# Projections over four PSUM banks, zeroing tied to the last norm, and an earlier retention in a two-layer hybrid transformer

## The chip, the cores and the metric

The kernel runs on one core of one Trainium2 chip. The metric is the device time of one execution in microseconds; the median of three runs is given. The engines are TensorE (PE, with its weight loads PEld), VectorE (DVE), ScalarE (ACT), GpSimd (POOL) and SyncE (SP, which here only issues loads and stores). Each engine runs its own instructions in the order in which they were laid down when the program was built; semaphores hold an instruction back until its inputs are there, and what stands behind it on that engine waits too.

## The reference

Two layers on 512 tokens of width 1024. Each layer mixes three kinds of attention and then runs a feed-forward part. Cut to its core:

```python
def hybrid_layer(x, attn_norm_w, w_in, ret_norm_w, kv_norm_w, w_uk, w_uv, w_out, mlp_norm_w, w_up, w_down, pos):
    h = rms_norm(x, attn_norm_w)
    proj = h @ w_in
    ret_cols, dsa_cols, dil_cols = jnp.split(proj, _offsets((RET_COLS, DSA_COLS, DIL_COLS)), axis=-1)
    mixed = jnp.concatenate([retention_mixer(ret_cols, ret_norm_w, pos),       # 4 heads, chunks of 128
                             dsa_mixer(dsa_cols, kv_norm_w, w_uk, w_uv),       # 4 heads, top-128 keys by an indexer
                             dilated_mixer(dil_cols)], axis=-1)                # 8 heads, three dilation patterns
    x = x + mixed @ w_out
    h = rms_norm(x, mlp_norm_w)
    return x + jnp.square(jax.nn.relu(h @ w_up)) @ w_down

def reference(x, ...):
    for layer in range(DEPTH):      # DEPTH = 2
        x = hybrid_layer(x, ...)
    return rms_norm(x, final_norm_w)
```

## The kernel before

**Arithmetic.** Every fp32 matrix is split into a high part (fp32r) and a low part (what the cast left over); a product is three fp32r matmuls: high by high, high by low, low by high. Weights are loaded in chunks of up to 512 KB (`dma`, line 248), cast on ScalarE (line 278) and their low part is taken on VectorE or GpSimd (line 286); there are three raw buffers and five finished ones. The feed-forward product with `w_down` is done with seven products in place of eight (`mlp`, line 949).

**Tokens.** The 512 tokens are four tiles of 128 (t = 0 to 3). `norm` (line 376) scales one tile: ScalarE squares it with a running sum (line 361), VectorE adds the two half sums (line 364), GpSimd raises the sum to the power -1/2 (line 368; the result is `r`), VectorE or GpSimd multiply (lines 383, 387, 389), TensorE transposes (line 352), and ScalarE and VectorE write high and low part of the activation (lines 399, 400). At the very start `start` (line 1060) loads the first norm's weight row and x tile 2, then the first constants, and then, in turn, weight chunks and the other x tiles, all on SyncE's queue. It runs the norms in the order 2, 3, 0, 1.

**PSUM.** There are eight banks: two called `mm` for projections and output parts, four called `at` for scores, transposes and attention values, two called `rt` for the retention and the feed-forward. A projection (`proj`, line 791) makes 24 matmuls into one `mm` bank, and VectorE and ScalarE copy the bank out (`evac_q`, `evac_k`: lines 423, 424, 436, 438; the high half of K also crosses partitions by a DMA that ScalarE issues, line 437). `dil_v` (line 537) makes the V of four dilated heads for the four token tiles: two tiles into `mm`, two into `rt`.

**The attention stage** (`attention`, line 830). First the projections that need tokens in rows and the latent (`token_parts`), then `zeros` (line 814), five GpSimd instructions that fill the retention's state and half of each of two K tiles with zeros, then the indexer, the first of 16 rounds of top-k on VectorE (lines 602, 603), and the first V. After that a loop over h = 0 to 12 issues the scores and softmax of head h (0 to 7 dilated, 8 to 11 sparse), one group of `FILL` (projections as filler: q and k of a pair, s for a sparse q, g for the retention's gates, d for the second V, r for the retention's q and k, v and w for the latent's k and v), from h = 9 on up to three output parts (`out_part`, line 892: 12 matmuls each with half of the rows of `w_out`), the values of head h - 1, a number of retention steps, and top-k rounds. `RET` (line 54) says how many of the retention's twelve steps follow each head: three steps for each token tile, the first with its scores (lines 659 to 679), the second with its products, state and norm (lines 681 to 733), the third with its gate (lines 735 to 742). `HOLD` (line 58) says from which of the eight output parts on they are kept for behind the loop. There the kept parts come, then the eight parts with the other half of `w_out`, and the next norm.

**What sets the order.** The program is handed to a scheduler that models each engine's time and takes, among the instructions that are ready, the one that comes first in program order, with the offsets of `PR` (line 72; a positive number means later). So filler moves into the holes that the scheduler sees, and each engine's order is fixed from then on.

**The end.** `final` (line 1047) norms one token tile of the last layer: one half on GpSimd (line 1052) and ScalarE (line 1054), the other on VectorE (line 1057); both halves are stored by SyncE (lines 1055, 1058). The tiles come in the order 2, 3, 0, 1.

Of the kernel before, what the change touches and what calls it, by code (L numbers as in the profile page):

```python
# [25 lines left out]
P = 128  # L26
# [26 lines left out]
    'FILL': 'q1,q2 k1 k2,g0,d g1,k3,q3 r,v s0,w,s1,',  # L53
    'RET': (0, 0, 0, 0, 0, 4, 0, 3, 0, 1, 3, 1, 0),
    'TOPK': (1, 1, 0, 4, 0, 10, 0),
    'POOL_LO': ('dv', 'o', 'sq', 'rg', 'rqk', 'dq', 'dk', 'ukv'),
    'LSPLIT': 2,
    'HOLD': 6,
    'KS': ((4, 6), (0, 2)),
# [64 lines left out]
class Kern:  # L124
# [251 lines left out]
    def norm(self, t, wb, act, room, first=False, h0=0):  # L376
# [4 lines left out]
        if not first:  # L381
            c0, c1 = halves[0]
            nc.gpsimd.tensor_tensor(hn[:, h0], self.x[t][:, c0:c1], wb[:, c0:c1], op=ALU.mult)
        r = self.norm_stats(t, None, halves)
        for h in (h0, 1 - h0):
            if h == h0 and not first:
                nc.vector.tensor_scalar(hn[:, h], hn[:, h], r[:, 0:1], None, op0=ALU.mult)
            else:
                nc.vector.scalar_tensor_tensor(hn[:, h], self.x[t][:, h * 512:(h + 1) * 512], r[:, 0:1],
                                               wb[h] if first else wb[:, h * 512:(h + 1) * 512], op0=ALU.mult,  # L390
                                               op1=ALU.mult)
            ps = self.at()
            for k in range(4):
                self.tr(ps[:, k * P:(k + 1) * P], hn[:, h, k * P:(k + 1) * P])
            psv = ps.rearrange("p (k c) -> p k c", k=4)
            for g in range(2):
                dst = act[h * 2 + g]
                hi = dst[:, 0, :, t * P:(t + 1) * P]
                nc.scalar.copy(hi, psv[:, 2 * g:2 * g + 2])
                nc.vector.tensor_tensor(dst[:, 1, :, t * P:(t + 1) * P], psv[:, 2 * g:2 * g + 2], hi.bitcast(F32),  # L400
                                        op=ALU.subtract)
# [135 lines left out]
    def dil_v(self, L, act, g):  # L537
        us = [(self.unit((L, "dv", g, k)), (k, k + 1, k + 2, k + 3)) for k in (0, 4)]
        for t in range(NT):
            ps = self.mm() if t < 2 else self.rt_bank()  # L540
            self.tform(us, act, t, ps, 256)
# [240 lines left out]
    def latent_k(self, L, pr):  # L782
# [6 lines left out]
        return self.evac_k(ps)  # L789

    def proj(self, key, act, cols=P):
        ps = self.mm()
        self.wform(self.unit(key), act, cols, ps, cols)
# [20 lines left out]
    def zeros(self):  # L814

        z = lambda o, a: self.nc.gpsimd.tensor_scalar(o, a, 0.0, 0.0, op0=ALU.mult, op1=ALU.add)
        z(self.sv.rearrange("p a c -> p (a c)"), bc(self.ident, [[0, 4], [1, P]]))
        for i in range(4):
            o = slice(64, 128) if i % 2 == 0 else slice(0, 64)
            z(self.kl[i // 2][o, i % 2, :], bc(self.ident[o], [[0, 4], [1, P]]))  # L820

# [8 lines left out]
    def attention(self, L, act):  # L830
        nc = self.nc
        A = self.A
        sc = None
        self.rt = [self.t(self.pmix, [P, 2, 1024], F32, "mix") for _ in range(2)]
        self.vd, self.sg, self.ct, self.vs, self.rqk_done = {}, None, None, None, False
        self.masks = self.t(self.psc, [P, N_CST - N_C1], F32, "masks")
# [63 lines left out]
        for h in range(12 + C["SK"]):  # L900
# [20 lines left out]
            if h >= C["SK"]:  # L921
                with self.prio("hv", h):
                    self.head_v(heads[(h - C["SK"]) // 2], (h - C["SK"]) % 2)
            for _ in range(C["RET"][h] if h < 13 else 0):
                with self.prio("ret", h):
# [121 lines left out]
    def final(self, t, wb, pool, junk):  # L1047
# [6 lines left out]
        nc.scalar.activation(xs, xs, AF.Copy, scale=r[:, 0:1])  # L1054
        nc.sync.dma_start(self.out[t * P:(t + 1) * P, c0:c1], xs)
        o = self.x[t][:, d0:d1]
# [3 lines left out]
    def start(self):  # L1060
        nc = self.nc

        row = self.t(self.pt, [P, 2 * S], F32, "PT")
        nc.sync.dma_start(row[0:1, :], self.A["attn_norm_w"][0].rearrange("(o c) -> o c", o=1))
        self.x[2] = self.t(self.pv, [P, D], F32, "xv")
# [64 lines left out]
```

## Time and profile before

| | |
|---|---|
| median of 3 runs | 1236.36 us (1236.02 to 1240.37) |
| the profiled execution: device time | 1236.08 us |
| its span, first to last instruction | 1234.1 us |
| busy: TensorE, VectorE, ScalarE, GpSimd | 98%, 75%, 55%, 38% of the span |
| mean granted TensorE clock | 0.997 |

Layer 0's attention stage runs from the start to about 291 us, its feed-forward to 618; layer 1's end at about 898 and 1226. Times are microseconds from the span's start. In a timeline row the first number is the start, the second the time from the first start to the last end of the merged instructions, and the bracket at the end is the idle time before them and what ended it. A matmul counts as busy from its start to its modelled end, so that neighbours overlap.

### The profile page before, as it was taken

The page shows a single profiled execution, that of the slowest core. Times are in us where ns is not written, and L with a number is a line of the kernel's source. Part 1 is how long each engine was busy: PE and PEld are TensorE (multiplying, and loading weights), DVE is VectorE, ACT ScalarE, POOL GpSimd, SP SyncE. Part 2 cuts the span into 40 slices and gives each one's busy share as a digit, 9 for nine tenths or more (in the row PEclk, how much of TensorE's full clock was granted, in tenths as well). Part 3 has the DMA queues.
Part 4 walks back from the last instruction along what each step waited for, and adds up shares of the span by engine and source line. Part 5 has one row for each costly group of instructions (what it writes and reads, how often), then busy time and mean ns, then how long its engine had stood idle before and what let it go on. Part 6 is the DMA issues. An engine that isn't in the chain of part 4 may idle for free.

```text
span 1234.1 us, 16904 instructions
## 1 busy us (share of the span) xinstructions
PE 1207.2 (98%) x6116; PEld 1027.6 (83%) x6116; DVE 921.4 (75%) x1582; ACT 679.2 (55%) x1241; POOL 472.4 (38%) x461
## 2 busy tenths in 40 slices
PE   7999999999999999999999999999999999999997
PEld 5988888889888888888889888888898888888886
DVE  5599957776875966858866997687769668587596
ACT  6645758745644535535566456686465354354454
POOL 3453748553412304214224546664534032140232
PEclk9999999999999999999999999999999999999999
DMA  7432324215244061260153323231180622514201
GB/s 217 120 83 72 95 69 121 86 53 188 85 137 137 1 215 58 69 184 16 35 166 102 95 71 96 91 120 53 52 256 1 205 68 69 176 30 140 82 1 69
DMA packets 142180, 122.73 MB, mean 99 GB/s; under 512 B 6801, under 2 KB 114065, under 8 KB 142098
## 3 DMA queue, kind: packets, MB, share of 16 engines
q1 hardware_dynamic: 140178, 118.52, 31.9%
q10 hardware_dynamic: 1920, 3.15, 1.0%
q8 instruction: 48, 0.79, 0.3%
q14 instruction: 34, 0.28, 0.1%
HBM read 114.31 MB, written 4.19 MB: 96 GB/s over the span
## 4 chain that ended last, share of the span: by engine, by line
PE 85%; DVE 12%; ACT 1%; issue 1%; DMA 1%; SPq 0%; POOL 0%; POOLq 0%; DVEq 0%; ACTq 0%
PE mm L336 35%; PE mm L348 15%; PE rt L1036 14%; PE at L1036 7%; PE mm L1036 3%; DVE sc L603 3%; DVE top L602 3%; PE at L352 2%; PE at L491 2%; PE at L444 1%; PE at L443 1%; DVE ph L462 1%; PE at L336 1%; DVE Q L424 1%; DMA raw<-in_w_in_dram 1%
## 5 line engine op out<-in xcount | busy, mean ns | idle before, releaser
L336 PE MATMUL mm<-act,w 128*128 128x512 f32 (+2 forms) x2352 | 516.1, 377 | 3.1 <-DVE Q L424 3.1
L336 PEld LDWEIGHTS mm<-act,w 128*128 128x128 f32 x2352 | 424.4, 188 | 79.8 <-issue 3.9
L286 POOL TENSOR_TENSOR w<-raw,w 128x512 fp32r<-128x512 f32 (+1 forms) x124 | 160.0, 1313 | 99.2 <-ACT w L278 74.0
L278 ACT CAST w<-raw 128x1024 fp32r<-128x1024 f32 (+1 forms) x138 | 142.9, 1037 | 79.2 <-PE rt L1036 27.6
L1036 PE MATMUL rt<-w,U 128*128 128x512 f32 x768 | 183.2, 389 | 0.0
L286 DVE TENSOR_TENSOR w<-rd,w 128x1024 fp32r<-128x1024 f32 x112 | 144.7, 1304 | 50.0 <-ACT w L278 50.0
L286 DVE TENSOR_TENSOR w<-raw,w 128x1024 fp32r<-128x1024 f32 (+1 forms) x76 | 94.0, 1238 | 107.5 <-ACT w L278 107.2
L1036 PEld LDWEIGHTS rt<-w,U 128*128 128x128 f32 x768 | 144.1, 188 | 29.9
L993 POOL TENSOR_TENSOR st<-s 128x256 f32<-128x256 f32 x32 | 39.1, 1223 | 330.1 <-ACT s L982 325.3
L278 ACT CAST w<-rd 128x1024 fp32r<-128x1024 f32 x112 | 117.6, 1050 | 83.4 <-PE rt L1036 41.7
L348 PE MATMUL mm<-w,act 128*128 128x456 f32 (+2 forms) x576 | 118.4, 351 | 3.0 <-DVE act L400 1.8
L348 PEld LDWEIGHTS mm<-w,act 128*128 128x128 f32 x576 | 96.4, 189 | 15.2 <-DVE act L400 2.8
L348 PE MATMUL mm<-w,mix 128*128 128x512 f32 x384 | 97.3, 401 | 0.6 <-DVE Q L424 0.5
L1036 PE MATMUL at<-w,U 128*128 128x512 f32 (+1 forms) x396 | 97.7, 386 | 0.0
L304 DVE TENSOR_TENSOR rd<-rd,rd 128x1024 f32<-128x1024 f32 x64 | 94.3, 1473 | 0.5
L1036 PEld LDWEIGHTS at<-w,U 128*128 128x128 f32 x396 | 73.6, 188 | 15.0
L980 ACT ACTIVATE s<-mm 128x512 f32<-128x512 f32 x62 | 36.9, 595 | 84.2 <-PE mm L336 74.5
L348 PEld LDWEIGHTS mm<-w,mix 128*128 128x128 f32 x384 | 70.5, 190 | 15.2 <-DVE Q L424 0.9
L997 ACT CAST U<-st 128x1024 fp32r<-128x1024 f32 x32 | 33.7, 1054 | 80.9 <-POOL st L994 80.9
L991 POOL TENSOR_TENSOR st<-s,s 128x256 f32<-128x256 f32 x32 | 36.7, 1146 | 92.0 <-ACT s L982 92.0
L463 ACT ACTIVATE ph<-ph,sm 128x128 f32<-128x128 f32 (+1 forms) x96 | 53.9, 562 | 24.5 <-DVE sm L462 23.8
L998 DVE TENSOR_TENSOR U<-s,U 128x256 fp32r<-128x256 f32 x64 | 63.9, 998 | 0.0
(169 smaller groups left out, 1766.4 us busy)
## 6 DMA issues: line engine op xcount, KB each, us to landing
raw<-in_w_up_dram SPq DMA_DIRECT2D x64, 512.0 KB, 4.2
rd<-in_w_down_dram SPq DMA_DIRECT2D x32, 1024.0 KB, 5.1
raw<-in_w_in_dram SPq DMA_DIRECT2D x48, 512.0 KB, 3.9
raw<-in_w_out_dram SPq DMA_DIRECT2D x16, 512.0 KB, 3.9
xv<-in_x_dram SPq DMA_DIRECT2D x7, 512.0 KB, 4.8
KH<-KH ACTq DMA_DIRECT2D x24, 128.0 KB, 2.3
raw<-in_w_in_dram SPq DMA_DIRECT2D x8, 256.0 KB, 2.9
xd<-xv SPq DMA_DIRECT2D x4, 512.0 KB, 3.9
```

The lines of the kernel that those rows point to most:

```text
L278: self.nc.scalar.copy(hi, src)
L286: eng.tensor_tensor(lo[:, i:i + step], src[:, i:i + step], hi[:, i:i + step].bitcast(F32), op=ALU.subtract)
L304: sub = lambda o, a, b: self.nc.vector.tensor_tensor(o, a, b, op=ALU.subtract)
L336: self.nc.tensor.matmul(ps[:cols, toks[0]:toks[1]], a, b, start=(k == 0 and j == 0), stop=(k == KB - 1 and j == 2))
L348: self.nc.tensor.matmul(ps[:, :w], a, b, start=(n == 0), stop=(n == tot - 1))
L463: nc.scalar.activation(p, p, AF.Exp, bias=a, scale=-1.0, accum_out=b)
L602: nc.vector.max(m, sc[b])
L603: nc.vector.match_replace(sc[b], m, sc[b], SENT)
L980: nc.scalar.activation(s, ps, AF.Relu)
L993: tt(st[:, 2], a[:, 0], a[:, 1], op=ALU.subtract)
L998: nc.vector.tensor_tensor(lo, src, hi.bitcast(F32), op=ALU.subtract)
L1036: nc.tensor.matmul(ps[:, c0:c1], a, w, start=(new and n == 0), stop=(n == 11), skip_group_check=True)
```

## The change

Six edits:

- Projections and the dilated V take their bank from a new counter: every third and fourth of four takes an `rt` bank, the others an `mm` bank, as long as no retention step has been issued in this layer.
- The zeroing of the K halves and of the state multiplies by `r` of the last norm and by zero, in place of multiplying by 0 and adding 0. So it can't start before that `r` is there.
- `RET`: the last five retention steps stand behind heads 8, 8, 9, 9 and 10, in place of 9, 10, 10, 10 and 11.
- `HOLD`: four of the eight first output parts are kept for behind the last head, in place of two.
- In `final`, the first half of each tile is stored from ScalarE's queue.
- In `start`, the first norm's weight row is loaded from ScalarE's queue.

```diff
@@ -51,11 +51,11 @@
 C = {
     'FILL': 'q1,q2 k1 k2,g0,d g1,k3,q3 r,v s0,w,s1,',
-    'RET': (0, 0, 0, 0, 0, 4, 0, 3, 0, 1, 3, 1, 0),
+    'RET': (0, 0, 0, 0, 0, 4, 0, 3, 2, 2, 1, 0, 0),
...
-    'HOLD': 6,
+    'HOLD': 4,
@@ def norm
         r = self.norm_stats(t, None, halves)
+        self.last_r = r
@@ def dil_v
-            ps = self.mm() if t < 2 else self.rt_bank()
+            ps = self.bank()
@@ def proj
+    def bank(self):
+
+        self.nbank += 1
+        return self.rt_bank() if self.nbank % 4 in (3, 0) and not self.ret_started else self.mm()
+
     def proj(self, key, act, cols=P):
-        ps = self.mm()
+        ps = self.bank()
@@ def zeros
-        z = lambda o, a: self.nc.gpsimd.tensor_scalar(o, a, 0.0, 0.0, op0=ALU.mult, op1=ALU.add)
+        z = lambda o, a, r=slice(0, P): self.nc.gpsimd.tensor_scalar(o, a, self.last_r[r, 0:1], 0.0, op0=ALU.mult,
+                                                                     op1=ALU.mult)
         z(self.sv.rearrange("p a c -> p (a c)"), bc(self.ident, [[0, 4], [1, P]]))
         for i in range(4):
             o = slice(64, 128) if i % 2 == 0 else slice(0, 64)
-            z(self.kl[i // 2][o, i % 2, :], bc(self.ident[o], [[0, 4], [1, P]]))
+            z(self.kl[i // 2][o, i % 2, :], bc(self.ident[o], [[0, 4], [1, P]]), o)
@@ def attention
+        self.nbank, self.ret_started = 0, False
...
+            self.ret_started = self.ret_started or C["RET"][h] > 0
             for _ in range(C["RET"][h] if h < 13 else 0):
@@ def final
-        nc.sync.dma_start(self.out[t * P:(t + 1) * P, c0:c1], xs)
+        nc.scalar.dma_start(self.out[t * P:(t + 1) * P, c0:c1], xs)
@@ def start
-        nc.sync.dma_start(row[0:1, :], self.A["attn_norm_w"][0].rearrange("(o c) -> o c", o=1))
+        nc.scalar.dma_start(row[0:1, :], self.A["attn_norm_w"][0].rearrange("(o c) -> o c", o=1))
```

## Rows read from the trace of the kernel before

**Rows 1.** Page, part 1: busy time, share of the span, instructions.

```profile
PE 1207.2 (98%) x6116; PEld 1027.6 (83%) x6116; DVE 921.4 (75%) x1582; ACT 679.2 (55%) x1241; POOL 472.4 (38%) x461
```

**Rows 2.** Stretches: length, busy time of PE, PEld, DVE, ACT, POOL, granted clock, DMA, GB/s.

```profile
0.00:20.00 20.00, 11.54 (x39) 7.84 (x40) 11.32 (x21) 13.68 (x32) 10.56 (x16) 1.00 0.92 279
80.00:140.00 60.00, 57.56 (x320) 49.62 (x319) 59.20 (x182) 33.40 (x70) 27.34 (x28) 1.00 0.33 90
210.00:264.00 54.00, 52.50 (x305) 44.39 (x304) 43.09 (x115) 36.15 (x83) 30.77 (x36) 1.00 0.26 81
264.00:272.00 8.00, 6.53 (x45) 5.41 (x44) 5.56 (x11) 4.16 (x10) 4.00 (x5) 1.00 0.23 67
292.00:612.00 320.00, 319.97 (x1481) 267.66 (x1481) 235.73 (x230) 157.78 (x211) 84.98 (x70) 1.00 0.34 104
870.00:878.00 8.00, 6.79 (x37) 5.54 (x36) 5.29 (x11) 2.85 (x7) 3.02 (x5) 0.80 0.23 66
```

**Rows 3.** Waits of PE: waiter, what ended the wait, total us, times, longest.

```profile
PE at L352 <- DVE Q L389: 4.7, 1, 4.7
PE mm L336 <- DVE Q L424: 3.1, 2, 1.6
...
PE rt L352 <- DVE rw L733: 1.5, 2, 0.7
PE rt L673 <- ACT rT L664: 1.3, 2, 0.7
PE mm L348 <- DVE KL L438: 1.2, 2, 0.6
PE rt L673 <- DVE rT L665: 1.1, 2, 0.5
```

**Rows 4.** Timeline of the start, DVE, POOL and PE: start, time, instruction.

```profile
5.23 0.16 DVE L364 SCALAR_TENSOR_TENSOR sm<-sm 128x1 f32<-128x1 f32 x1 [3.82 <-ACT P L361]
...
6.21 2.66 POOL L816 TENSOR_SCALAR KL<-cst 64x512 fp32r<-64x512 f32 x4
...
8.84 0.55 POOL L368 TENSOR_TENSOR sm<-sm,pw 128x1 f32<-128x1 f32 x1
...
9.42 1.89 POOL L383 TENSOR_TENSOR Q<-xv,ph 128x512 f32<-128x512 f32 x1
...
17.69 3.57 PE L348 MATMUL mm<-w,act 128*128 128x456 f32 x16 [1.33 <-DVE act L400]
...
34.15 0.74 POOL L657 TENSOR_TENSOR rv<-mix,rv 128x256 fp32r<-128x256 f32 x1 [13.70 <-ACT rv L656]
```

**Rows 5.** Line 824, the loads of x tiles 3, 0 and 1.

```profile
DMA to landing us min/median/max: 5.2/5.3/5.5
```

**Rows 6.** Timeline around the longest bank wait of layer 0.

```profile
87.05 0.69 DVE L424 SCALAR_TENSOR_TENSOR Q<-mm,Q 64x512 fp32r<-64x512 f32 x1
...
87.89 2.30 PE L336 MATMUL mm<-act,w 128*128 128x512 f32 x9 [1.57 <-DVE Q L424]
```

**Rows 7.** Timelines of the last retention tile, in layer 0 and in layer 1.

```profile
265.98 0.58 ACT L664 CAST rT<-rt 128x512 fp32r<-128x512 f32 x1 [0.27 <-PE rt L352]
...
271.53 0.48 PE L690 MATMUL rt<-sv,rT 128*128 128x256 f32 x2
...
874.72 2.84 PE L348 MATMUL mm<-w,mix 128*128 128x512 f32 x6
```

**Rows 8.** The chain that ended last: start, time, a feed-forward block.

```profile
375.04 43.52 PE mm L336 x192
```

**Rows 9.** Line 437's issues on ScalarE; then the end's timeline.

```profile
L437 ACTq DMA_DIRECT2D KH<-KH x24: 468/468/536, 88.0 to 815.3; - x24
...
1228.30 2.47 SPq L1055 DMA_DIRECT2D out_dram<-s  x2
...
1229.70 0.75 DVE L1057 SCALAR_TENSOR_TENSOR xv<-xv,sm,wb 128x512 f32<-128x512 f32 x1 [0.73 <-POOL sm L368]
1230.87 0.38 SPq L1058 DMA_DIRECT2D out_dram<-xv  x1
```

## The prediction

> **What bounds the kernel now.** I began with the busy shares [rows 1]: TensorE is busy 1207.2 of 1234.1 us, so at most 27 us can be had without taking work away, and the change takes none from TensorE. The table of stretches [rows 2] says where those 27 us lie. In the feed-forward stretch 292 to 612 TensorE is busy 319.97 of 320, and nothing in the change touches it. The first 20 us have 8.5 us of idle TensorE. In layer 0's attention stage, 80 to 140 has 2.44 idle while VectorE is at 59.20 of 60, 210 to 264 has 1.5, and 264 to 272 has 1.47, together 5.4; layer 1's stage is a near copy (870 to 878 is shown: 1.21, at a clock of 0.80), so some 11 us lie there, and the rest in the output at the end.
>
> Then the list of what TensorE waited for [rows 3]. Three kinds matter: 4.7 us once for the first normalised x tile (VectorE line 389); 3.1 + 1.2 us, in two waits each (one a layer), for the evacuation of a projection's PSUM bank (lines 424 and 438); and 1.5 + 1.3 + 1.1 us for the retention's own steps (lines 733, 664, 665). The timelines behind each [rows 4, 6, 7] tell which edit meets which wait. A shown wait is a little short of the loss: after the wait that ends at 87.89 [rows 6] the matmul also pays its restart.
>
> **The start: zeroing moved behind the norms.** At the start the sum of squares of x tile 2 is ready on VectorE at 5.23 + 0.16 = 5.4 us, but GpSimd's power for it starts at 8.84 [rows 4]. Between stand the five zeroings of line 816 (four of them take 2.66 us from 6.21, the first fills the time before), which went first because they need only a constant. In the new kernel each zeroing reads r, the last thing that the last norm makes, so on GpSimd's queue they come after the fourth power. The first power can then start at about 5.5, 3.3 us earlier, and with it lines 389, the transposes and the casts of tile 2. What the moved work lands on: after the fourth power GpSimd sat idle for 13.70 us, until line 657 at 34.15 [rows 4], so 3.3 us there cost nothing; who reads the zeroed halves are score and state matmuls far behind. If that cover were gone, the price would be the 3.3 us on line 657. In layer 1 the same five run when nothing waits for them, before and after: 0.
>
> What is late next? GpSimd took up tile 3 at 9.42 [rows 4], and a load of x takes 5.3 us from its issue [rows 5]. Tile 3's is the eighth issue on SyncE; eight at 0.4 to 0.5 us end at 3.2 to 4.0, so it landed at 8.5 to 9.3 and was held by the zeroing for less than 1 us. TensorE runs without a break only from 17.69 [rows 4]. So I can't count all 3.3 to 4.7 us: tile 2's 24 projection matmuls, 5 us of work, can move into the hole before 17.69 only as their weight chunks land. The bounds are 0 (the weights and tiles 0, 1 set the pace anyway) and -4.7 (the whole wait). I take **-2.5**, about half, since one of four tiles is freed and three are bound by their loads.
>
> The weight row's load moves from SyncE's queue to ScalarE's. An issue on ScalarE costs 0.47 us (line 437's median), one on SyncE about 0.38 (line 1058) [rows 9]. Every load behind it, x tile 2 first, is issued 0.4 us earlier; ScalarE waits for that tile anyhow, so its own 0.47 us are covered. **-0.4**, bounds -0.5 and 0.
>
> **Four projection banks.** Projections took turns on two banks; now every third and fourth takes one of the retention's two, until the retention starts at head 5. Each layer's waits of this kind come before that: one at 86 to 88, where the third projection waits until VectorE, busy with top-k, has copied out the first (line 424 from 87.05, matmul at 87.89) [rows 6], the other for line 438. In the new turn order the third projection takes a bank that nothing holds. All of 3.1 + 1.2 = 4.3 us can go [rows 3]. Against that: VectorE is busy 59.20 of 60 us in 80 to 140 [rows 2], so every copy-out is as late as before, and a TensorE that runs ahead meets the next result of VectorE earlier. Bounds -5 (the waits with their restarts) and 0. I take two thirds, **-2.9**, since TensorE has seven more projections and four V tiles ahead of the retention to run ahead with. The retention finds its two banks free at head 5: the last projection on them is a gate, two projections earlier.
>
> **Retention earlier, four parts kept.** The last five of the twelve retention steps stood at heads 9 (one), 10 (three) and 11 (one); they move to 8 (two), 9 (two) and 10 (one). In the old trace the last tile's scores run when no head is left: from line 664 (265.98) to the last product of line 690 (over at 272) [rows 7], with 1.47 us idle in layer 0 and 1.21 in layer 1 [rows 2]. The 1.3 + 1.1 us of lines 664 and 665 [rows 3] are these waits. Earlier they lie beside head work, while behind the last head four parts of 12 matmuls (48 at 43.52/192 = 0.227 us [rows 8], 10.9 us) are kept instead of two. I take **-2.7** (1.47 + 1.21). The line 733 wait (1.5 us) belongs to head 7's steps, which don't move: 0. Layer 1's six matmuls at 874.72 took 2.84 us [rows 7] where six at full clock take 1.4; that clock dip followed the same idle that layer 0 had at full clock [rows 2], so it may go but I don't count it: 0, bound -1.4. On the other side, heads 9 and 10 lose two parts, 24 x 0.227 = 5.4 us of filler a layer, and gain retention waits; bounds -4.1 and +10.8 (both layers' filler missed in full).
>
> **The end.** The last two results are ready together (line 1057 from 1229.70 for 0.75, and ScalarE's beside it); SyncE issues one by 1230.77 and the other from 1230.87 [rows 9]. On two queues the second goes 0.4 us earlier. But tile 3's and tile 0's output issues now stand on ScalarE, 0.47 us each, ahead of the last tile's squares. I take **-0.2**, bounds -0.4 and +0.5.
>
> **The sum.** -2.5 - 0.4 - 2.9 - 2.7 - 0.2 = -8.7 us on the profiled execution's 1236.08 gives 1227.4; the runs' median lies 0.28 above that execution, so 1227.7. The scheduler lays out every queue anew, so small waits will stand elsewhere; this is inside the range. About 0.5%, 6.2 us, is what can be told from no change: below 1230.2 is faster, above 1242.5 slower.
>
> **The rivals.** *VectorE takes the banks' gain back.* If TensorE, 2 us ahead, just waits for VectorE's scores or for its KL and Q copies later in the same 80 us, the bank term is 0, and the earlier arrival also moves filler away from the retention, whose term halves: 1236.36 - 2.9 - 1.35 - 0.2 = 1231.9. For it: VectorE at 59.20 of 60 [rows 2]. Against: the stage as a whole is TensorE's, which idles there only 2.44.
> *Filler runs out at heads 9 and 10.* This ends slower. The retention now has its waits at heads 8 to 10, where there are 5.4 us less of output parts a layer to cover them. In full that costs 10.8 us and loses the retention's gain: 1236.36 - 2.9 - 2.9 - 0.2 + 10.8 = 1241.2. It decides against the change once more than 3.0 us a layer are idle beyond today's. For it: already 1.5 us idle in 210 to 264 [rows 2]. Against: the kept parts are ready from head 9 on, and a scheduler that sees a hole can pull them in.
> *The start doesn't move:* loads, not GpSimd, set it. 1227.7 + 2.5 = 1230.2. For it: tile 3's take-up right at its landing [rows 4, 5].
> *The clock.* Row: after 1.2 us of idle in 8 the granted clock there was 0.80, with a stretch at the lower level, 1.2 GHz [rows 2, 7]; each such dip costs 1.4 us. A dip for each of the four waits that the change breaks up would give 1227.7 + 5.6 = 1233.3. The Trainium skill (TensorE: Matmul & The Clock Gate, "A second HAM failure mode: psum-queue depth-cycling") tells of a kernel whose turns through PSUM banks left small idles in which the clock fell again and again, which speaks against more banks. The trace bears that out little: 80 to 140, with longer waits, kept 1.00 [rows 2].
>
> **Chances.** Forecast 0.55 (1227.7; its own range 1221 to 1232), VectorE 0.25, filler 0.10, start 0.07, clock 0.03. Faster by over 0.5%: 0.47 of the forecast, half of the start's 0.07, and 0.03 of the others, 0.54. Slower by over 0.5% is the filler case beyond its price: 0.04. The rest, 0.42, is within. The range: all bounds in the change's favour give -4.7 - 0.5 - 5 - 4.1 - 0.4 = -14.7, 1221.7, taken as 1221.5; upward it takes in the VectorE and clock cases and the cheaper half of the filler case, to 1237.
>
> **What would show it.** First power on GpSimd near 5.5 and TensorE unbroken well before 17.69: start right. No wait for line 424 or 438 ahead of head 5, and the idle in 80 to 140 under 1 us: banks right; the same idle ended by score or PT results: VectorE's case. 264 to 272 without line 664 and 665 waits, and the idle of 210 to 264 no more than 1.5: retention right; 4 us or more there: filler. Two last output issues side by side: end right. The forecast is wrong if the start gains under 1 us while the banks give nothing back.

## The result: slower by 0.65%, with the start's gain in it

The changed kernel takes 1246.15 us (median of 11 executions, 1239.78 to 1248.5) against 1236.36 (11, 1234.9 to 1240.72): a ratio of 1.0065, 95% interval 1.0046 to 1.0084. The prediction was 1227.7, with a range that ended at 1237. The profiled execution took 1246.15 us, its span is 1244.4.

The page's part 1 of the changed kernel: busy time, share of the span, instructions.

```profile
PE 1217.3 (98%) x6116; PEld 1033.2 (83%) x6116; DVE 918.4 (74%) x1582; ACT 680.1 (55%) x1241; POOL 476.3 (38%) x461
```

TensorE has the same 6116 matmuls as in [rows 1] and is busy 10 us longer. The page counts 27.1 us of idle TensorE where it was 26.9, so the loss is not plain idle time alone: some matmuls ran longer. The table of stretches shows where (length, busy time of PE, PEld, DVE, ACT, POOL, granted clock, DMA share, GB/s).

```profile
0.00:20.00 20.00, 15.12 (x56) 10.47 (x57) 12.57 (x24) 14.14 (x32) 8.76 (x13) 1.00 0.93 280
80.00:140.00 60.00, 56.65 (x308) 48.83 (x307) 59.07 (x184) 32.81 (x69) 25.83 (x27) 0.97 0.32 85
210.00:264.00 54.00, 51.68 (x295) 43.07 (x293) 38.52 (x108) 34.94 (x81) 30.66 (x35) 1.00 0.25 78
264.00:272.00 8.00, 6.93 (x37) 5.69 (x37) 5.64 (x13) 3.85 (x8) 1.74 (x2) 0.79 0.22 71
302.00:612.00 310.00, 309.97 (x1418) 258.63 (x1417) 229.11 (x217) 153.28 (x201) 80.80 (x66) 1.00 0.33 102
880.00:892.00 12.00, 10.92 (x49) 9.15 (x49) 7.20 (x16) 4.18 (x10) 4.81 (x6) 0.72 0.01 1
```

Against [rows 2]: the start has 56 matmuls in its first 20 us and not 39, busy 15.12 and not 11.54. 80 to 140 lost 0.91 us of busy time and 12 matmuls. 264 to 272 issued 37 matmuls where there were 45, at a granted clock of 0.79 in place of 1.00, and layer 1's copy of it, now at 880 to 892, ran at 0.72 (before: 0.80 in 870 to 878). The feed-forward is as dense as before.

To follow this through the span I use one figure, worked out from the trace. **Excess** is the time from one matmul's start to the next one's, less the median of that time for the matmul's shape, summed over a stretch; it holds waits and lost clock together. Of the 10.3 us that the span grew, excess explains nearly all: the start -2.9; layer 0, 80 to 140: +3.0 and 260 to 320: +4.6; layer 1, 860 to 920: +4.5; all other stretches, about +1 together.

What TensorE waited for in the changed kernel (total us, times, longest). Lines behind 384 stand one lower in the file than before (from the projections on it is more), so line 425 is before's 424.

```profile
PE at L492 <- ACT PT L486: 3.7, 7, 1.1
PE rt L348 <- DVE P L646: 2.9, 2, 1.5
...
PE at L352 <- DVE Q L390: 2.2, 2, 2.0
...
PE mm L348 <- DVE Q L425: 1.1, 2, 0.5
...
PE rt L674 <- DVE rT L666: 0.8, 2, 0.4
```

The bank waits of [rows 3] for lines 424 and 438 have shrunk, as the retention's have. In their place stand two others: the attention values wait for the cast of their transposed weights (line 486; 1.0 us before, as line 485), and, new, a V tile on an `rt` bank waits for the gate's copy (line 646).

### The profile page after: what moved, and what is told of

Same layout as the page of the kernel before. It is cut to its first block, busy times and chain, and to the rows that moved or that the text cites. A ratio compares the mean times of both kernels' runs of the same rounds, so it can differ in the third digit from the quotient of the medians.

```text
span 1244.4 us, 16862 instructions
## 1 busy us (share of the span) xinstructions
PE 1217.3 (98%) x6116; PEld 1033.2 (83%) x6116; DVE 918.4 (74%) x1582; ACT 680.1 (55%) x1241; POOL 476.3 (38%) x461
## 5 line engine op out<-in xcount | busy, mean ns | idle before, releaser
L336 PE MATMUL mm<-act,w 128*128 128x512 f32 (+2 forms) x2160 | 472.1, 376 | 0.0
L336 PEld LDWEIGHTS mm<-act,w 128*128 128x128 f32 x2160 | 389.1, 188 | 69.3
```

The costliest lines, as they stand in the source:

```text
L336: self.nc.tensor.matmul(ps[:cols, toks[0]:toks[1]], a, b, start=(k == 0 and j == 0), stop=(k == KB - 1 and j == 2))
```

## The experiments

Eighteen kernels ran, each beside the kernel before on the same chip (its medians there: 1236.06, 1236.46, 1237.2, 1237.56, 1238.39). "Parts" counts the output-part matmuls (line 348 on `mix`) that TensorE runs in layer 0 ahead of the last head's last score matmul; "last head" is the time from that matmul to that head's last value product. Both are read from each kernel's one profiled execution. In 17 and 18 a part of the computation is left out.

| kernel | median us | ratio to before (95%) | parts | last head us |
|---|---|---|---|---|
| before | 1236 to 1238 | | 64 | 19.8 |
| changed | 1246.15 | 1.0065 (1.0046 to 1.0084) | 48 | 28.3 |
| 1 banks | 1250.41 | 1.0106 (1.0083 to 1.0129) | 48 | 27.3 |
| 2 RET and HOLD | 1242.54 | 1.0050 (1.0031 to 1.0069) | 64 | 23.6 |
| 3 start and end | 1233.95 | 0.9978 (0.9963 to 0.9993) | 64 | 19.8 |
| 4 changed, old RET and HOLD | 1247.39 | 1.0087 (1.0063 to 1.0112) | 48 | 27.3 |
| 5 banks, projections only | 1255.5 | 1.0138 (1.0100 to 1.0175) | 48 | 27.3 |
| 6 banks, V tiles only | 1246.66 | 1.0078 (1.0053 to 1.0103) | 48 | 27.3 |
| 7 HOLD only | 1244.33 | 1.0051 (1.0033 to 1.0069) | 64 | 23.5 |
| 8 scores' buffer | 1243.33 | 1.0049 (1.0028 to 1.0071) | 86 | 14.4 |
| 9 V tiles, order laid back | 1238.22 | 0.9997 (0.9983 to 1.0012) | 64 | 19.8 |
| 10 banks, order laid back | 1241.8 | 1.0034 (1.0020 to 1.0047) | 64 | 19.8 |
| 11 q1, q2, start, end | 1247.89 | 1.0081 (1.0049 to 1.0113) | 64 | 19.8 |
| 12 HOLD 8, start, end | 1243.83 | 1.0051 (1.0031 to 1.0071) | 64 | 19.8 |
| 13 one priority alone | 1248.48 | 1.0087 (1.0070 to 1.0105) | 48 | 27.3 |
| 14 q1, start, end | 1240.85 | 1.0023 (1.0012 to 1.0034) | 64 | 19.8 |
| 15 zeroing only | 1235.47 | 0.9985 (0.9977 to 0.9994) | 64 | 19.8 |
| 16 start and end again | 1234.54 | 0.9980 (0.9969 to 0.9991) | 64 | 19.8 |
| 17 half the top-k rounds | 1244.94 | 1.0063 (1.0044 to 1.0081) | 48 | 27.3 |
| 18 the same with banks | 1243.02 | 1.0046 (1.0031 to 1.0060) | 48 | 27.3 |

### Which edit costs (1 to 4)

Each takes the edits of the diff named in the table and leaves the others out.

> The kernel before with the four projection banks alone. Theory A (the banks are taken back on the spot by VectorE, and dear at the gate): the 1.7 us wait for line 424 near 86 is gone, but between 100 and 140 TensorE idles some 3 to 4 us more than before, waiting for the copy of the gate's bank (line 646 in after) and for PT casts; the time is 1238 to 1241. Rival (the banks are sound, the loss comes from the retention's new place alone): no such wait, 1231 to 1234. Second rival (projections run early are missed as filler behind the heads): the idle between 260 and 282 doubles as in after, 1242 to 1246.

> The kernel before with the new places of the retention steps and four kept parts alone. Theory B (the scheduler spends the kept parts as filler earlier, so the last head's values and the last retention tile run without filler): the stretch behind the last score matmuls shows about 4 us more idle in each layer, with the clock down in it; 1242 to 1246. Rival (that loss needs the banks): the stretch is as before, 1234 to 1238.

> The kernel before with the zeroing behind the norms and the two DMA edits alone. If the start's gain read off the trace of after (TensorE does 56 matmuls in the first 20 us in place of 39) is real and kept: 1232 to 1234. Rival (given back in the stretch where VectorE is full, 60 to 140): 1236 to 1237.

> The changed kernel with the old places of the retention steps and two kept parts: banks, zeroing and DMAs stay. If theory B holds and A too: 1236 to 1239 (what is left is the banks' cost less the start's gain). If the loss behind the heads comes from the banks: still 1243 to 1247.

The banks alone cost 14 us, more than any of the three theories gave them; retention and kept parts alone cost 6.5; the start and end gain 2. The costs don't add: with the banks in (4), old or new `RET` and `HOLD` make no difference that shows. That speaks for a common cause behind both, and doesn't prove one.

### Which half of each edit (5 to 8)

```diff
 # 5: projections as in the change, V tiles keep their banks      # 6: the other way round
-            ps = self.bank()
+            self.nbank += 1
+            ps = self.mm() if t < 2 else self.rt_bank()
...
 # 8: in ret_tile, before's kernel
-            pm = self.rwork()
+            pm = self.work()
```

> Before plus half of the banks edit: the projections q1, q2, g0, g1 take the rt banks as in after, and the V tiles of the dilated heads keep their old banks (0 and 1 on mm, 2 and 3 on rt). With the whole edit alone the kernel took 1250.4 against 1236.4. Theory V (the two V tiles that sat on rt were work that TensorE could take up while the two mm banks were full; moving them and interleaving products takes that filler away from 110 to 135 us): most of the loss goes with the V tiles, so this one takes 1232 to 1239, the wait of 1.7 us at 86 gone and 100:140 idle no more than before. Rival G (a gate's result sits on an rt bank until VectorE comes to its copy behind the top-k rounds): the loss is here, 1243 to 1250, with a matmul of a V tile on rt waiting for a gate's copy.

> Before plus the other half: the V tiles of the second dilated group take rt, mm, mm, rt as in after, and every projection stays on mm. Theory V: the loss is here, 1242 to 1250, idle time of TensorE between 100 and 140 of 4 us or more in each layer. Rival G: 1235 to 1239, idle between 100 and 140 as before (1.6 us by excess over dense spacing).

> Before with only HOLD 4 in place of 6 (four output parts left for behind the last head... the first four of eight are handed out before it). Together with the moved retention steps it took 1242.5 against 1236.1. Theory H (the retention's places change nothing, since its tiles start at the same times to 0.2 us; what costs is that the parts are no longer there beside the last retention tile and the last head): 1240 to 1244, TensorE's excess between 260 and 280 of 5 us or more against 2.8 before. Rival R (the moved steps cost): 1235 to 1238, excess as before.

> Before, with one buffer changed: the retention's masked scores (256 columns, two a tile) take a buffer of the common work pool (3 buffers) in place of the pool of two that also holds a tile's output until its gate. Theory B (these two buffers and the chain of norm and gate behind them set the pace of 25 to 27 us from tile to tile, not the heads at which the steps are handed out): the second to fourth tiles start 3 to 8 us earlier each and the layer's end gains 0 to 4 us, 1229 to 1237 in all. Rival P (the pace is set by TensorE's own queue order, behind heads and filler): tile starts within 1 us of before's 188.2, 215.4, 241.0, 265.3, time 1235 to 1238. Rival W (the common pool is what then waits: the heads' copies come later): slower, 1238 to 1245.

5 and 6 answered neither theory: both halves cost, 19 and 10 us, and their sum is twice the whole. Kernel 6 is the telling one. Its excess between 80 and 140 is 3.4, as before, so the banks do no harm where they are used; but from 260 to 280, some 120 us behind the last V tile, it is 8.3 against 2.8 (with lost clock in it, of which more below). Kernel 7 has all of 2's loss, so the moved retention steps cost nothing; they gain nothing either, since the four tiles start at 188.4, 215.6, 241.2 and 265.2 us in kernel 2 and at 188.2, 215.4, 241.0 and 265.3 before. Theory H held. In 8 the tiles start 28.0, 53.1 and 77.5 us after the first, before 27.2, 52.8 and 77.1: Theory B fell, and what sets this pace is left open. But 8 too costs 7 us, a time that Rival W had named; whether its buffers are the reason was not looked at.

So edits that have little in common (projections' banks, V tiles' banks, kept parts, a buffer) all cost, and a large part of it at the end of the attention stage. What most of them share shows in the column of parts. In kernels 1, 4, 5, 6 and the changed one, TensorE's laid-out order of the last 100 us of the stage is another one: 16 of the output-part matmuls that stood ahead of the last head's scores now stand behind them, and the last head with its chain of scores, softmax, transposes and values takes 27 us in place of 20 (of these 7 us the 16 parts themselves, at 0.227, are 3.6). In 1, 4, 5 and 6 nothing was edited there. The scheduler lays out the whole stage from modelled times, and what it finds free depends on all that went before. In kernel 6 the first difference behind the first retention tile, but for one value product a few places off at 193 us, is one product (line 786, the second key of the sparse pairs), laid a few instructions earlier than in before, at 202 us; much of what follows falls otherwise.

### The order as the suspect (9 to 13)

Kernels 9, 10 and 13 change one number of the priority table, which moves no buffer and no bank. In 9 and 10 it was picked so that TensorE's instructions from the first retention tile on stand in before's order again (over the matmuls of layer 0's trace from that tile on, the displacements against before sum to 2740 places in kernel 6 and to 78 in 9, to 2742 in kernel 1 and to 142 in 10). In 13 that one product's priority is changed in the kernel before, so that up to the first retention tile the order is before's and from there on it is the one of kernel 6 (18 places off).

```diff
 # 9:  kernel 6 with
-'hs_7': 800
+'hs_7': 100
 # 10: kernel 1 with
-'hv_8': 400
+'hv_8': -200
 # 13: the kernel before with
-'fill_w': 100
+'fill_w': -800
```

> The kernel with the V tiles' banks alone (1246.7 against 1236.5), and one entry of the priority table changed (hs_7, 800 to 100), which lays TensorE's instructions from the first retention tile on (188 us) in the order that they have in before, but for a few that stand one or a few places off. Banks as there. Theory O (the edit costs because the scheduler, which lays the instructions out once for the whole layer, gives the last 80 us another order, in which the output parts stand ahead of the last head and the last retention tile and not between them): the loss goes, 1235 to 1239, excess between 260 and 280 back from 8.3 to 2.5 to 4. Rival S (the banks themselves are late in the end part, or buffers): 1244 to 1249 as without the priority.

> The kernel with the whole banks edit alone (1250.4), with one entry of the priority table changed (hv_8, 400 to -200) so that TensorE's order from the first retention tile on is before's again but for a few places. Theory O: the part of the loss after 180 us goes (some 4 us of excess and 1 to 2 us of lost clock per layer), that at 100 to 140 us stays (3 us per layer): 1239 to 1244. Rival S: 1248 to 1252. A third outcome, 1233 to 1237, would mean that the loss at 100 to 140 is given back later.

> Before with one entry of the priority table alone (fill_w, 100 to -800; the second key product of the two sparse pairs is laid out earlier). No bank, no buffer, no retention step and no kept part is changed; TensorE's instructions from the first retention tile on then stand as in the kernels with the banks edit, but for a few. Theory O (it is this order of the end part that costs): 1243 to 1249, last score at 241 to 243 us, excess from the last head's score to its last product near 3.8 against 0.9, retention tiles 27 us apart. Rival S (banks and buffers cost, order is innocent): 1234 to 1239.

In time Theory O held each time. Laid back, the V tiles' banks cost nothing (0.9997, 0.9983 to 1.0012) and the whole banks edit 4.6 us in place of 14; and the order alone, with no other edit, costs 11 us. One expectation was missed: the excess of kernel 9 from 260 to 280 was to fall to 2.5 to 4, and it is 6.7.

The reason of that miss is the clock, which differs between executions of one program. Stretch 262 to 282 in kernel 9:

```profile
262.00:282.00 20.00, 18.80 (x82) 15.64 (x81) 12.66 (x25) 5.71 (x14) 9.20 (x11) 0.74 0.18 51
```

TensorE idles less here than in before's profile (1.2 against 1.5 us), but at a clock of 0.74. Kernels 3, 15 and 16, whose end part has before's order place for place, show 0.74, 0.83 and 0.83 there, with 1.2 us idle. So the clock of this stretch doesn't follow from the order alone, and what one profile shows of it, or of the excess there, can't be laid to the order.

A figure to which the clock adds little is the time from the first retention tile's first matmul to the last value product (layer 0 is at 1.00 up to 264 us in every profile). TensorE runs 434 matmuls in it, 114 of them parts, in every kernel but the changed one, 2, 7 and 8. Where 64 parts stand ahead of the last scores it takes 76.1 to 76.6 us, in both layers of eight kernels, the one before among them; where 48 do, 80.1 to 80.4, in both layers of seven. Kernel 14 has one layer of each kind: 76.6 and 80.3. So this order costs some 3.7 us a layer by its waits. (The changed kernel takes 81.3 and 80.1 us, for 440 matmuls; 2 and 7 take 80.4, for 452.) In 9 and 11, which have `hs_7` at 100, the time is half a us shorter than in before; that priority was not run alone.

What the order does shows in kernel 13's timeline of TensorE around the retention's last tile (start, time, engine, line, tiles, shape, count, idle before and what ended it):

```profile
263.40 0.69 PE L491 MATMUL at<-PT,vs 128*128 128x384 f32 x4
263.93 0.29 PE L352 MATMUL at<-cst,ph 128*128 128x128 f32 x1
265.05 0.38 PE L491 MATMUL at<-PT,vs 128*128 128x256 f32 x1 [0.82 <-ACT PT L485]
265.67 2.36 PE L348 MATMUL mm<-w,mix 128*128 128x512 f32 x9 [0.24 <-DVE xv L828]
...
269.54 0.44 PE L491 MATMUL at<-PT,vs 128*128 128x384 f32 x1 [0.28 <-ACT PT L485]
270.43 1.31 PE L491 MATMUL at<-PT,vs 128*128 128x384 f32 x5 [0.45 <-DVE PT L486]
...
273.23 0.32 PE L673 MATMUL rt<-rT 64*128 64x128 f32 x1 [0.68 <-ACT rT L664]
274.08 1.65 PE L673 MATMUL rt<-rT 64*128 64x128 f32 x11 [0.53 <-DVE rT L665]
275.67 2.93 PE L348 MATMUL mm<-w,mix 128*128 128x512 f32 x6
```

And in the kernel before:

```profile
264.12 0.97 PE L491 MATMUL at<-PT,vs 128*128 128x384 f32 x6
...
266.62 0.32 PE L673 MATMUL rt<-rT 64*128 64x128 f32 x1 [0.68 <-ACT rT L664]
267.47 1.05 PE L673 MATMUL rt<-rT 64*128 64x128 f32 x11 [0.53 <-DVE rT L665]
268.45 1.66 PE L348 MATMUL mm<-w,mix 128*128 128x512 f32 x6
```

The last tile's waits for its rT casts are the same in both. What the new order adds are the last values' waits for their PT casts, 0.82, 0.28 and 0.45 us, with nine parts between the first and the others and none behind them until 275.67. Then six part matmuls take 2.93 us, as in [rows 7] at the lower clock, where before's six take 1.66. HOLD takes parts away from the same place by its own way. Line 348 alone, 265 to 272 us, first in the kernel before, then in kernel 7 (length, busy time and count of these matmuls, clock):

```profile
265.00:272.00 7.00, 1.81 (x7) 1.00 0.24 69
```

```profile
265.00:272.00 7.00, 0.00 (x0) 0.81 0.25 71
```

The last retention tile starts at 265.3 in both. Before, seven part matmuls stand between its steps; with HOLD 4 none does, though 114 have run by the last value product in both. The clock is 0.81 here; kernels 15 and 16, with before's order, ran at 0.71 and 0.63 in 264 to 272, so this isn't shown to be HOLD's work. The whole of 262 to 282, in the kernel before and in the changed one:

```profile
262.00:282.00 20.00, 18.53 (x102) 15.41 (x101) 16.26 (x34) 7.65 (x20) 9.88 (x12) 1.00 0.18 51
```

```profile
262.00:282.00 20.00, 17.79 (x87) 14.65 (x86) 14.46 (x32) 8.49 (x20) 7.53 (x9) 0.83 0.18 53
```

Less than 1 us more is idle, and 15 fewer matmuls are done: most of this stretch's loss between these two executions is clock, and kernels 3, 9, 15 and 16 show that before's order can lose as much there.

```diff
 # 11: start, end, hs_7 at 100, and only q1 and q2 by bank(); k, gates and V tiles keep their banks
 # 12: start, end, and
-    'HOLD': 6,
+    'HOLD': 8,
```

> The start's and end's edits (1234 alone), and of the banks edit only the queries q1 and q2 on the rt banks: gates and V tiles keep theirs; hs_7 at 100, which keeps TensorE's order of before from the first retention tile on. Theory G2 (of the projections it is the two gates on rt whose copies stand behind the top-k rounds that make the wait at 100 to 140): that stretch has before's excess of 1.6 us, the wait of 1.7 us at 86 is gone in both layers, 1228 to 1233. Rival I (it is the side-by-side order of products on two pairs of banks, queries included): excess of 3 to 5 us between 100 and 140, 1235 to 1241.

> The start's and end's edits (1234 alone) with HOLD 8 in place of 6: the other way from the change, no part of the first pair of output products is kept for behind the last head. HOLD 4 cost 7.9 us, 5.2 of them... by excess 4.5 us in the first layer and 3 in the second, beside lost clock. Theory O (a new order of the last 80 us is rarely as good as the one there was, whichever way it is turned): slower than 1234 by 2 to 9 us. Rival M (fewer parts left is better, since parts beside the last retention tile fill its waits): 1228 to 1233.

Both are misses for the hopeful side, and 11 lies above both its ranges. In 12 the other direction of HOLD costs over 9 us against start and end alone (3, 16), somewhat more than Theory O gave, and in another place than it named: up to the last value product its figures are before's (64 parts, 76.6 us). What it lacks is the kept parts behind it. Stretch 282 to 300 in before and in 12, and 12's longest wait there, for the last retention tile's norm:

```profile
282.00:300.00 18.00, 17.97 (x123) 16.23 (x123) 13.32 (x26) 11.12 (x25) 7.92 (x7) 1.00 0.54 151
```

```profile
282.00:300.00 18.00, 15.16 (x91) 13.33 (x89) 11.72 (x24) 9.02 (x19) 8.12 (x8) 0.91 0.39 115
```

```profile
PE rt L352 <- DVE rw L734: 4.5, 2, 2.3
```

In 11 the end part kept its order, and the loss came in the middle. Its first two waits:

```profile
PE mm L348 <- DVE Q L425: 6.7, 2, 3.4
PE at L444 <- DVE sm L463: 4.1, 2, 2.0
```

In each layer 3.4 us (in layer 0 from 163 us) and 2 us (from 130), both for VectorE. Theory G2, which blamed the gates, fell; the queries alone do it.

### The middle: banks against VectorE (14, 17, 18)

```diff
 # 14: start, end, and of the banks edit one projection
-        ps = self.mm()
+        ps = self.rt_bank() if (key[1], key[2]) in (('dq', 1),) else self.mm()
 # 17, 18: before, and before with the banks edit, both with
-    'TOPK': (1, 1, 0, 4, 0, 10, 0),
+    'TOPK': (1, 1, 0, 2, 0, 4, 0),
```

> The start's and end's edits (1234 alone), and of the banks edit one projection, q1, on an rt bank: the smallest edit that takes away the wait at 86 us. TensorE's order from the first retention tile on is before's but for a few places; between 86 and 140 us it is not, since the scheduler opens the next product before q1 is through. Theory O for the middle (each bank more opens products side by side, and the one that is waited for ends later): excess from 80 to 140 of 2 to 4 against before's 3.4, 1231 to 1236. Rival G2 (only q2, gates and V tiles did harm): excess 1.6 or less, 1228 to 1231.

> Before with 8 of the 16 rounds of top-k left out (so the sparse heads attend to other keys; this is part of the computation left out). It is the base for the next kernel: VectorE, busy 59.2 of 60 us in 80 to 140, gets some 20 us of room there. If VectorE's late copies make TensorE's waits at 86 and 130 (theory V1), the excess from 80 to 140 falls from 3.4 to under 1.5; if not, it stays at 3 to 3.5.

> The same with the whole banks edit. With all rounds the banks edit raised the excess from 80 to 140 from 3.4 to 4.9 (8.4 to 8.9 idle and lost clock in both layers). Theory V1 (the first rival: more banks only move TensorE's wait from one late result of VectorE to the next): with room on VectorE the excess from 80 to 140 is under 1.5 with the banks too, and no more than without them. Theory I (it is the order of the products opened side by side, whatever VectorE does): 4 or more here against under 2 without the banks.

In 14 the wait at 86 us is gone, and another stands at 107 to 109, for the very same kind of copy:

```profile
109.09 3.10 PE L348 MATMUL rt<-w,act 128*128 128x256 f32 x24 [2.43 <-DVE Q L425]
```

1.6 us were taken away and 2.4 came back. The excess from 80 to 140 is 4.4 (expected 2 to 4), and layer 1's end part was laid out anew in the bargain (48 parts ahead of the last scores there), so the time missed the expected 1231 to 1236 by 5 us.

17 and 18 point to the reason. Stretches 80 to 100 and 100 to 140, first without top-k's second half and without the banks, then with the banks:

```profile
80.00:100.00 20.00, 18.42 (x85) 15.19 (x84) 19.67 (x57) 9.06 (x17) 9.76 (x8) 1.00 0.43 122
100.00:140.00 40.00, 40.00 (x243) 35.68 (x243) 23.29 (x77) 26.46 (x58) 19.71 (x22) 1.00 0.29 78
```

```profile
80.00:100.00 20.00, 20.00 (x94) 16.78 (x93) 19.73 (x58) 6.28 (x10) 9.96 (x8) 1.00 0.49 139
100.00:140.00 40.00, 39.48 (x240) 34.72 (x239) 24.13 (x77) 29.54 (x68) 19.59 (x22) 1.00 0.25 70
```

And the same with all rounds, before and with the banks alone (1):

```profile
80.00:100.00 20.00, 18.43 (x86) 15.19 (x85) 19.67 (x56) 9.05 (x17) 9.57 (x8) 1.00 0.46 123
100.00:140.00 40.00, 39.13 (x236) 34.44 (x236) 39.54 (x127) 24.34 (x53) 17.77 (x20) 1.00 0.27 74
```

```profile
80.00:100.00 20.00, 20.00 (x93) 16.78 (x92) 19.73 (x58) 6.44 (x11) 9.81 (x8) 1.00 0.51 138
100.00:140.00 40.00, 36.63 (x222) 31.80 (x221) 39.59 (x125) 26.37 (x58) 16.07 (x18) 1.00 0.24 68
```

In 80 to 100 the banks give 1.6 us in both pairs. In 100 to 140, with VectorE at 39.5 of 40, they lose 2.5; with VectorE at 24 of 40 they lose 0.5. So with room on VectorE the banks gain 1.06 us of busy time in layer 0. Layer 1 doesn't repeat the gain. By excess from 20 us (in layer 1 from 645) to the first retention tile, the banks take the two layers from 3.6 and 3.7 us to 5.5 and 7.1 with all rounds, and from 2.5 and 1.4 to 1.6 and 1.7 with half of them: a cost of 5.3 us in all, against a gain of 0.6. The medians, 1244.94 and 1243.02, are of four and five executions whose ranges overlap. That is Theory V1's outcome. It is not its proof: with fewer rounds the scheduler also lays the middle otherwise (between 80 and 186 us, 1054 places between 17 and before, 4116 between 18 and 1), so load and order changed together. The excess from 80 to 140 is 2.0 in 17 and 1.4 in 18; 17 was expected under 1.5, but the wait at 86 stands there still, with all its 1.6 us, while the one at 130 is gone.

Kernel 17 on its own is the study's oddest line: VectorE has less to do, the stretch from 100 to 140 is full, and the kernel is 6.5 us slower than before, with the 48 parts and the 27 us of kernel 13 at its end.

### The start, by its parts (15, 16)

> Before with the zeroing's edit alone. By the prediction's step the first V tile's wait goes with it: 2.5 us at the start, 1232.5 to 1235 in all; if the weight row's queue was what counted, 1235.5 to 1237 and the wait of TensorE for the first query's copy at 12 us stays at 4.7 us.

> The start's and end's edits together once more, on the chip of the two above, to be compared with them: 1232 to 1235.

The zeroing gives 2.1 us (0.7 to 2.8 by its interval), and the two queue edits perhaps 0.9 more. Kernels 3 and 16 are the best of this study, ahead of both the kernel before and the changed one.

## Why the prediction was wrong, point by point

**The start was right.** -2.5 was predicted for the zeroing, and kernel 15 measured -2.1. GpSimd and VectorE at the changed kernel's start:

```profile
4.86 0.16 DVE L364 SCALAR_TENSOR_TENSOR sm<-sm 128x1 f32<-128x1 f32 x1 [3.44 <-ACT P L361]
5.09 0.56 POOL L368 TENSOR_TENSOR sm<-sm,pw 128x1 f32<-128x1 f32 x1 [4.67 <-DVE sm L364]
...
7.79 1.11 DVE L286 TENSOR_TENSOR w<-raw,w 128x912 fp32r<-128x912 f32 x1 [1.35 <-ACT w L278]
8.82 0.74 DVE L390 SCALAR_TENSOR_TENSOR Q<-xv,sm,at 128x512 f32<-128x512 f32 x1
...
9.09 1.27 POOL L383 TENSOR_TENSOR Q<-xv,ph 128x512 f32<-128x512 f32 x1 [3.44 <-DMA xv<-in_x_dram]
...
9.61 1.11 PE L352 MATMUL at<-cst,Q 128*128 128x128 f32 x4 [2.00 <-DVE Q L390]
```

The power runs at 5.09 where [rows 4] had it at 8.84. Then two other things are late. Tile 2's second half (line 390 at 8.82) stands on VectorE behind a weight chunk (line 286), so TensorE still waits 2.00 us for it; and the next tile waits for its load, as was said: line 383 at 9.09 behind a DMA, against 9.42 before. These, not GpSimd, are the likely reason why 3.3 us earlier gave 2.1. The weight row's -0.4 is in line with the 0.9 us between kernels 15 and 16, which lies inside their scatter. The rival by which the start doesn't move fell.

**The end: no gain.** From TensorE's last matmul to the end of the span it is 6.81 us before and 6.90 after. The last two results are now issued side by side, from ScalarE and SyncE, and the end doesn't come earlier for it.

**Banks: the step that failed first.** -2.9 was predicted, with bounds of -5 and 0. The wait at 86 did go: in the changed kernel line 336 starts on `rt` at 83.36 without a wait, where VectorE's copy of the old bank runs at 84.26.

```profile
83.36 6.96 PE L336 MATMUL rt<-act,w 128*128 128x512 f32 x30
...
84.26 0.69 DVE L425 SCALAR_TENSOR_TENSOR Q<-mm,Q 64x512 fp32r<-64x512 f32 x1
```

But 47 us on, a V tile wants the `rt` bank that a gate's result still occupies, and VectorE comes to the gate's copy between two top-k rounds:

```profile
131.70 0.66 DVE L646 SCALAR_TENSOR_TENSOR P<-P,rt 128x512 f32<-128x512 f32 x1
...
132.41 1.80 PE L348 MATMUL rt<-w,act 128*128 128x256 f32 x9 [1.46 <-DVE P L646]
```

Before it, at 128.18, TensorE had waited 1.12 us for a PT cast. This is the first rival's mechanism (VectorE at 59.20 of 60, [rows 2]), and kernels 17 and 18 speak for VectorE's load as what decides. Its price was wrong: it put the bank term at 0, and with the order laid back (10) it is +4.6 us, which the excess ahead of the first retention tile bears out (5.4 and 7.0 us in 10's layers against 3.6 and 3.7). The bound of 0 excluded a loss without giving a reason. Why the new waits are longer than the old ones is argued, not shown: a TensorE that runs ahead spends its independent work early, and then stands in front of the late result with nothing left to do.

**"The scheduler lays out every queue anew, so small waits will stand elsewhere; this is inside the range."** This sentence is the costliest error: it puts the new order at nothing without a row. What is laid out anew isn't small: 10 of the banks' 14 us (kernels 1 and 10), and 9 of the V tiles' 10 (6 and 9), and 11 us from a priority alone (13). It lies 60 to 150 us behind the edit, where the bank term had counted nothing. The changed kernel itself was not run with its order laid back; it has the 48 parts of kernels 1 and 4 in both layers.

**Retention and HOLD.** -2.7 was predicted, and +6 to +8 measured (2, 7). Two steps failed. Moving the last five steps was to put the last tile beside head work; the tiles didn't move by more than 0.2 us (kernel 2), so the steps gained nothing. And the kept parts were to be 10.9 us of cover behind the last head; they stand behind the last retention tile, not in it. The waits for lines 664 and 665 did go (kernel 7 has none from 255 to 285 us), as the prediction's sign asked, but waits for the tile's next inputs (lines 678 and 679, 1.0 us) and for PT casts (0.6) stand in their place. The second rival had the sign and, with a price of up to 10.8 us, the size; its place was wrong. Heads 9 and 10 don't run dry: 210 to 264 is busy 51.68 in the changed kernel against 52.50, and as many part matmuls have run by the last value product (114 in kernels 2 and 7 as before). What is missing are the seven between the last tile's scores and products. The rival had a chance of 0.10.

**The clock.** The dip was costed at 0 and as a rival at 5.6 us with a chance of 0.03. In the profiled execution of before one stretch of the attention stages ran at the lower level, 1.2 GHz [rows 2, 7], in the changed kernel there are several: 0.97 in 80 to 140, 0.79 in 264 to 272, 0.72 in 880 to 892. Each of these stretches has waits in it, but kernels 3, 9, 15 and 16 fall to 0.74 to 0.83 in 262 to 282 with before's order and 1.2 us idle, so the dips are not shown to be the edits' work. The price of 1.4 us was too low: from the first retention tile to the last part matmul, layer 0 takes 101.8 us in before's profile and 106.0 in kernel 3's, with the same order. (It also set a length of 2.84 us against a spacing of 1.4; six parts at full clock have a length of 1.66.) Over executions of the changed kernel the mean granted clock runs from 0.990 to 0.997, and the time from 1248.5 to 1239.78, so some 8 us go with it; at 0.997, before's usual value, it takes 1239.8 and 1242.4 us, still 3 to 6 more than before. Read from this scatter, roughly half of the loss is waits and half is clock; no kernel here separates the two, and why the changed kernel falls to the lower clock more often than before is open. The Trainium skill (TensorE: Matmul & The Clock Gate, "A second HAM failure mode: psum-queue depth-cycling") tells of a kernel whose cycling through PSUM banks left small idles so often that the clock kept going between its two levels. The runs here bear this out little: the changed kernel had 0.97 in 80 to 140, but kernels 1 and 10, with the same banks, kept 1.00 there, and most of the lost clock lies at the end of the attention stage.

**The rivals were not exclusive.** VectorE, the missing filler and the clock were weighed as alternatives of which one would come. Something of all three came, and the sum was outside of every one of them. The sign that the prediction named for being wrong, a start that gains under 1 us, didn't come: the start was its sound part.

## What to carry to other kernels

Where a scheduler lays out a long stage from modelled times, an edit has two prices: the local one, which a profile can give, and that of the new order everywhere behind it, which was the larger one here for the banks. Before an edit is judged, compare each engine's laid-out order far behind it with the old one, lay it back (by a priority) and time again; and time one change of order without any edit, to learn what order alone is worth (here 11 us, more than the 8.7 that the change was to gain). Compare clocks over many executions, not in one profile. Banks added in front of VectorE, which was busy 59.2 of 60 us there, moved the wait to that engine's next late result.

## What was not expected

Less work made the kernel slower: without half of the top-k rounds VectorE was busy 23.29 of 40 us in place of 39.54, TensorE had no idle time in 100 to 140, and the kernel took 1244.94 us against 1238.39 (17); its end part has the order of kernel 6 (26 places off). And the same instructions in the same order scatter more than the edits are worth: kernel 3's executions run from 1230.88 to 1236.9 us, with the mean granted clock between 0.999 and 0.991. At the shortest they come within 3.2 us of what was predicted for the whole change.
